# A hybrid encoder layer on one core: twelve of the sixteen gate products in the input stage instead of seven

## The chip, the cores and the metric

The kernel runs on one core of one Trainium2 chip. The time is device microseconds of one execution. A core has a matrix engine (PE, its weight loads shown as PEld), three engines for elementwise work (DVE, ACT, POOL) and a sync engine (SP) that mainly starts DMA transfers. Each engine takes its own instructions strictly in the order in which the program lists them, and waits where an operand is not there yet.

## What is computed

One encoder layer over two sequences of 1024 and 256 tokens, 1280 columns in all, with model width 1024. From the normalized input `h` one wide product `h @ w_in` gives the inputs of three things: attention, a recurrent branch (a scan over tokens in both directions) and 2048 gate columns. The change concerns the gate columns.

```
p = h @ w_in[l]
p_mla, p_rwkv, p_gate = (columns of p)
o_mla = mla_branch(p_mla, ...) @ w_mla_o[l]
o_rwkv = rwkv_branch(p_rwkv, ...) @ w_rwkv_o[l]      # holds the scan over tokens
gm, gr = jnp.split(jax.nn.sigmoid(p_gate), 2, axis=-1)
x = x + g1 * ((gm * o_mla + gr * o_rwkv) @ w_out[l])
...                                                  # then a SwiGLU feed-forward layer
```

The 2048 gate columns are 16 products of 128 columns each (8 for `gm`, 8 for `gr`). Each product has 8 slices of the contracted dimension, and each slice is multiplied three times, because a number is split into a high and a low half: high by high, high by low, low by high.

## The kernel before

The stages follow one another on PE: the input products (gemm, L67), attention, the scan with other work laid into it, the merge of the two branches, and the feed-forward layer. The order of every engine's instructions is fixed when the program is built, by a scheduler that runs through an estimated timeline (`schedule_with_timeline_sim=True`); the source order and the pools of buffers are its input. The rows of an execution say how long that order really takes.

The gate products are made in two places, and a constant `NB` (L35) divides them:

- `gates` (L443), called at L1369 behind the input products, makes products 0 to NB-1 from `h` as it lies in SBUF. It goes through the columns in chunks of 512, 512 and 256 (`CH`), so a product has 24 matmuls of 512 columns twice and 24 of 256 columns: 72. All use one PSUM buffer (`gps`, one bank), which ACT empties with a tanh (L456) before the next chunk may begin. The weights come in two halves per product; each is loaded (L51), cast on ACT (`whi`, L53) and subtracted on POOL (`wlo`, L55).
- `phase_fill` (L1131) makes products NB to 15 beside the scan, with `product` (L1044, matmuls at L1054). There `h` is read back from DRAM in pieces of 256 columns (`x`), so a product has 5 x 24 = 120 matmuls of 256 columns, and its weights are loaded and split once for each pass over the columns, three times in all. When the gates are done, the same function multiplies the attention output by `w_mla_o` (`mla_out`: loads `om` and the row sums `rs` into `raw` and `bc`, splits them, multiplies, and writes `xm` to DRAM). All of this together is called the fill below.

```
js = range(NB, 16)
ws = weights(g, io["w_in"][20 + NB], KT)
...
both = js[:LAG] if len(xs) > 1 else []
for j in both:
    gate(j, *xs, ws=ws)
```

The scan (`phase_rwkv`, L714) has ten batches of 128 tokens, each with two steps of 64 (`step`, L918). A step is a chain through PE and back: `py` (L927), copies to `ru`, `py` again with an inverted block `tt` (L933), copies to `xv`, the state update `pS` (L939) and the output (L945). `prepare` (L968; matmuls `pA`, L819) and `solve`/`invert` (L851, L1009) make the blocks of later batches. Steps have the highest priority in the scheduler, the inversions a smaller one, the rest none. Behind the scan `merge` (L1104) reads `xm` and the gates back.

Of the kernel before, what the change touches and what calls it, by code (L numbers as in the profile page):

```python
# [31 lines left out]
    VEC[_n] = (_at, _w)  # L32
    _at += _w
NVEC = _at
NB = 7  # L35
SPN = ('kk',)
WV = (0, 1)
AB = 8
# [8 lines left out]
def split_w(g, src, kt, eng=None, tag="w", pool=None, width=P, rbufs=2, bufs=2):  # L47
    nc = g.nc
    pool = pool or g.wst
    raw = pool.tile([P, kt, width], F32, tag=tag + "raw", name="wraw", bufs=rbufs)  # L50
    nc.sync.dma_start(out=raw if len(src.shape) == 3 else raw.rearrange("p (d f) n -> p d f n", d=src.shape[1]), in_=src)  # L51
    hi = pool.tile([P, kt, width], F32R, tag=tag + "hi", name="whi", bufs=bufs)
    nc.scalar.copy(hi, raw)  # L53
    lo = pool.tile([P, kt, width], F32R, tag=tag + "lo", name="wlo", bufs=bufs)
    (eng or nc.gpsimd).tensor_tensor(lo, raw, hi, ALU.subtract)  # L55
    return hi, lo
# [386 lines left out]
def gates(g, hh, hl):  # L443

    nc, io = g.nc, g.io
    for j in range(NB):
        ws = [split_w(g, io["w_in"][20 + j][:, k0:k0 + 4, :], 4, pool=g.gp, tag="gw", rbufs=1) for k0 in (0, 4)]
# [592 lines left out]
def weights(g, src, kt):  # L1040
    return [split_w(g, src[:, k0:k0 + 4, :], 4, pool=g.fl, tag=g.ft, rbufs=RB, bufs=WB) for k0 in range(0, kt, 4)]
# [89 lines left out]
def phase_fill(g):  # L1131
# [23 lines left out]

    js = range(NB, 16)
    ws = weights(g, io["w_in"][20 + NB], KT)
    spans = [(0, 256), (512, 768), (1024,)]
# [313 lines left out]
```

## Time and profile before

| what | value |
|---|---|
| time, median of 3 runs | 2715.98 us (2709.65 to 2723.69) |
| the profiled execution: its own time | 2719.07 us |
| its span, first to last instruction | 2717.4 us |
| PE busy | 2547.4 us, 94% |
| DVE, ACT, POOL busy | 1326.4, 1020.0, 841.7 us (49%, 38%, 31%) |
| mean granted TensorE clock | 0.957 of full speed |

A share of busy time is a mean over stages with different limits, so the stages are looked at one by one. A busy PE is one whose pipelined matmuls overlap: a 512-column matmul is shown with about 390 ns, but the next one starts about 230 ns later, and it is the distance between starts that counts.

### The profile page before, as it was taken

The numbers are of one execution on the slowest core, as the hardware profiler recorded it, in microseconds if no ns is written. First come the engines' busy times: TensorE is split into PE (matmuls) and PEld (weight loads), VectorE is DVE, ScalarE is ACT, GpSimd is POOL, SyncE is SP. The second block draws the span as 40 slices with busy tenths as digits, with TensorE's granted clock in tenths as the row PEclk, the third lists the DMA queues.
The fourth block names the chain that finished last, engine by engine and source line by source line (L and its number), as shares of the span: only waits on it lengthen the run. The fifth ranks groups of instructions, "written<-read, shape, count | busy, mean of one in ns | idle before, by whom it ended". The sixth has DMA issues, their size and how long they took to land.

```text
span 2717.4 us, 47321 instructions
## 1 busy us (share of the span) xinstructions
PE 2547.4 (94%) x19578; PEld 2160.1 (79%) x19578; DVE 1326.4 (49%) x2138; ACT 1020.0 (38%) x1913; POOL 841.7 (31%) x824
## 2 busy tenths in 40 slices
PE   5999999989997899999998988999999999999997
PEld 3777778778886788988877767778888888888886
DVE  6665562367776374565646557462222222222228
ACT  4433333257676565565653233241110111101114
POOL 1112131011115455454634466342111111111123
PEclk8999999999998798998988989999999999999998
DMA  7655531110013334444445655221111110111113
GB/s 294 226 185 198 188 146 63 45 29 18 20 32 107 103 107 137 141 114 137 126 147 164 191 182 154 92 71 55 39 39 39 39 36 35 39 39 39 39 40 132
DMA packets 178120, 273.80 MB, mean 101 GB/s; under 512 B 15008, under 2 KB 104944, under 8 KB 177904
## 3 DMA queue, kind: packets, MB, share of 16 engines
q1 hardware_dynamic: 164512, 223.19, 25.8%
q0 software_dynamic: 5760, 26.22, 2.4%
q10 hardware_dynamic: 7632, 21.37, 2.3%
q8 instruction: 154, 2.52, 0.4%
q14 instruction: 62, 0.51, 0.1%
HBM read 202.52 MB, written 68.20 MB: 100 GB/s over the span
## 4 chain that ended last, share of the span: by engine, by line
PE 75%; DVE 11%; ACT 5%; DMA 4%; issue 3%; POOL 2%; SPq 0%; DVEq 0%; POOLq 0%; ACTq 0%
PE mm L67 42%; PE fp L1054 8%; PE s L626 3%; PE o L660 2%; PE gps L453 2%; PE pA L819 2%; PE proj L559 2%; PE t L647 2%; PE py L927 2%; DMA ld<-scr_s 1%; PE pS L939 1%; PE py L945 1%; PE lora L369 1%; PE ada_ps L170 1%; PE py L933 1%
## 5 line engine op out<-in xcount | busy, mean ns | idle before, releaser
L55 POOL TENSOR_TENSOR wlo<-wraw,whi 128x512 fp32r<-128x512 f32 (+3 forms) x233 | 406.5, 1748 | 1177.6 <-ACT whi L53 1166.7
L53 ACT CAST whi<-wraw 128x512 fp32r<-128x512 f32 (+2 forms) x248 | 194.5, 789 | 898.0 <-issue 466.7
L67 PE MATMUL mm<-h2h,whi 128*128 128x512 f32 (+1 forms) x1056 | 279.2, 358 | 2.9 <-ACT whi L53 2.9
L67 PE MATMUL mm<-h2h,wlo 128*128 128x512 f32 (+1 forms) x1056 | 278.4, 357 | 1.1 <-POOL wlo L55 1.1
L67 PE MATMUL mm<-h2l,whi 128*128 128x512 f32 (+1 forms) x1056 | 278.2, 357 | 0.0
L67 PE MATMUL mm<-g,whi 128*128 128x512 f32 (+1 forms) x1056 | 240.6, 359 | 6.2 <-DVE ft L1259 5.6
L1054 PE MATMUL fp<-x,whi 128*128 128x256 f32 (+1 forms) x912 | 211.1, 324 | 11.7 <-ACT x L1036 5.0
L67 PEld LDWEIGHTS mm<-g,whi 128*128 128x128 f32 x1056 | 177.8, 190 | 38.0 <-issue 5.7
L67 PEld LDWEIGHTS mm<-h2h,whi 128*128 128x128 f32 x1056 | 177.1, 189 | 34.6 <-ACT whi L53 3.4
L67 PEld LDWEIGHTS mm<-h2h,wlo 128*128 128x128 f32 x1056 | 176.8, 188 | 32.7 <-POOL wlo L55 2.0
L67 PEld LDWEIGHTS mm<-h2l,whi 128*128 128x128 f32 x1056 | 176.9, 188 | 31.2 <-issue 0.5
L1271 DVE SCALAR_TENSOR_TENSOR x<-mm,g2h,x 128x512 f32<-128x512 f32 (+1 forms) x144 | 87.0, 655 | 196.3 <-PE mm L67 196.0
L1054 PEld LDWEIGHTS fp<-x,whi 128*128 128x128 f32 x912 | 157.6, 206 | 23.9 <-ACT x L1036 6.1
L67 PE MATMUL mm<-hl,whi 128*128 128x512 f32 (+1 forms) x480 | 147.5, 364 | 7.7 <-DVE hl L265 7.7
L67 PE MATMUL mm<-hh,whi 128*128 128x512 f32 (+1 forms) x480 | 148.1, 366 | 6.4 <-ACT pp L320 3.8
L1054 PE MATMUL fp<-x,wlo 128*128 128x256 f32 (+1 forms) x456 | 147.8, 325 | 6.3 <-POOL wlo L55 6.3
L1259 DVE SCALAR_TENSOR_TENSOR ft<-ft,mm 128x512 f32<-128x512 f32 (+1 forms) x66 | 36.0, 594 | 225.6 <-ACT ft L1258 225.6
L67 PE MATMUL mm<-hh,wlo 128*128 128x512 f32 (+1 forms) x480 | 145.8, 363 | 0.0
L1260 DVE TENSOR_TENSOR ft<-ft,mm 128x512 f32<-128x512 f32 (+1 forms) x66 | 36.0, 593 | 217.5 <-PE mm L67 217.5
L67 PE MATMUL mm<-g,wlo 128*128 128x512 f32 (+1 forms) x528 | 136.2, 359 | 1.4 <-POOL wlo L55 1.4
L626 PE MATMUL s<-kb,q 128*128 128x512 f32 (+1 forms) x432 | 112.0, 392 | 2.3 <-ACT pr L632 2.2
L67 PEld LDWEIGHTS mm<-hh,whi 128*128 128x128 f32 x480 | 84.5, 191 | 27.8 <-issue 6.9
(331 smaller groups left out, 5239.2 us busy)
## 6 DMA issues: line engine op xcount, KB each, us to landing
wraw<-in_w_ffn_in_dram SPq DMA_DIRECT2D x56, 512.0 KB, 3.5
wraw<-in_w_in_dram SPq DMA_DIRECT2D x68, 256.0 KB, 3.6
araw<-in_w_ada_dram ACTq DMA_DIRECT2D x32, 512.0 KB, 3.6
wraw<-in_w_ffn_out_dram SPq DMA_DIRECT2D x26, 512.0 KB, 3.6
wraw<-in_w_in_dram SPq DMA_DIRECT2D x20, 512.0 KB, 3.8
x<-scr_h SPq DMA_DIRECT2D x20, 512.0 KB, 7.5
araw<-in_w_ada_dram SPq DMA_DIRECT2D x16, 512.0 KB, 9.3
gt<-scr_gate SPq DMA_DIRECT2D x32, 256.0 KB, 2.7
```

The source lines that it names most:

```text
L53: nc.scalar.copy(hi, raw)
L55: (eng or nc.gpsimd).tensor_tensor(lo, raw, hi, ALU.subtract)
L67: nc.tensor.matmul(p[:, :n], lhsT=ww[:, k, :], rhs=aa[:, k, c0:c0 + n], start=(k == 0 and i == 0), stop=(k == kt - 1 and i == 2))
L453: nc.tensor.matmul(p[:, :n], lhsT=ww[:, k % 4, :], rhs=aa[:, k, c0:c0 + n], start=(k == 0 and i == 0), stop=(k == KT - 1 and i == 2))
L559: nc.tensor.matmul(p[:, :n], lhsT=ww[:, k, :], rhs=aa[:, k, c0:c0 + n], start=(k == 0 and i == 0), stop=(k == kt - 1 and i == 2))
L626: nc.tensor.matmul(s[:, o:o + w], lhsT=a[:, tt * P:(tt + 1) * P], rhs=b[:, c0 + o:c0 + o + w], start=(m == 0), stop=(m == 2))
L647: nc.tensor.transpose(t[:, j, :], prs[i][:, kk * P:(kk + 1) * P], g.ident)
L660: nc.tensor.matmul(o, lhsT=vs[h // 4][:, c0 // P + kk, h % 4, :], rhs=pts[j][m][kk // 4][:, kk % 4, :], start=(kk == 0 and m == 0), stop=( ...
L819: nc.tensor.matmul(pA[e][:, pt], lhsT=bk[HV[e], 2 * pt + sl], rhs=lt[HV[e], pt, e], start=True, stop=True)
L927: nc.tensor.matmul(py[e][HV[r], c, :], lhsT=lt[:, HV[r]], rhs=xv[:, u, e, :], start=(u == 0), stop=(r == 0 and u == 7))
L1054: g.nc.tensor.matmul(p[:, c:c + n], lhsT=ww[:, k % 4, :], rhs=aa[:, k, :n], start=(k == 0 and i == 0), stop=(k == kt - 1 and i == 2))
L1271: nc.vector.scalar_tensor_tensor(x1[:, dt, c0:c0 + n], p[:, :n], g.g2h[:, dt, c0 // TP:c0 // TP + 1], x1[:, dt, c0:c0 + n], ALU.mult, ALU.add)
```

## The change

```
-NB = 7
+NB = 12
```

Products 7 to 11 leave `phase_fill` and are made in `gates`. No other line is touched. In the changed program `gates` has 360 more matmuls (5 x 72) and `phase_fill` 600 fewer (5 x 120). What follows shows where the scheduler put them.

On SP, at the end of the input stage, between the tables for the attention keys (`ktab`) and queries (`qtab`), stand the weight loads of the last gate products:

```order
 L481 DMA ktab<-in_ktab_dram 64x1024
 L482 DMA ktab<-in_ktab_dram 64x256
-L51 DMA wraw<-in_w_in_dram 128x512 x3
+L51 DMA wraw<-in_w_in_dram 128x512 x13
 L538 DMA qtab<-in_qtab_dram 128x1024
 L51 DMA wraw<-in_w_uq_dram 128x384
```

Ten loads are added in one place, two for each of the five products. On PE the same holds: the last run of L453 matmuls ahead of attention had 144 in a row, which is two products, and now has 504, which is seven; all the earlier ones stand where they stood.

On PE, in the second step of the scan's sixth batch (`tt` is the inverted block, `py` and `pS` the step's products, `pA`, `pT`, `pv` those of `prepare`, `pz` of `invert`), the rows before are:

```order
L819 MATMUL pA<-lt,bk 128x128 x8
L832 MATMUL pT<-cst,bk 128x128 x4
L1054 MATMUL fp<-x,whi 128x256 x2
L927 MATMUL py<-xv,lt 64x64 x32
L840 MATMUL pv<-cst,ld 128x128 x4
L1054 MATMUL fp<-x,wlo 128x256
L1054 MATMUL fp<-x,whi 128x256 x2
L1054 MATMUL fp<-x,wlo 128x256
```

The same step in the changed program:

```order
L819 MATMUL pA<-lt,bk 128x128 x8
L832 MATMUL pT<-cst,bk 128x128 x4
L927 MATMUL py<-xv,lt 64x64 x32
L840 MATMUL pv<-cst,ld 128x128 x4
L840 MATMUL pv<-cst,vr 128x128 x4
L878 MATMUL pz<-xr,aa 32x16 x11
L933 MATMUL py<-ru,tt_8102 64x64 x8
```

The fill is gone from this step, and from every later one: in the changed program the last matmul of the fill (gates and `mla_out` together) stands just ahead of L933 in the first step of the sixth batch, while before it goes on to the end of the scan. Up to there the two programs have much the same number of fill matmuls in each step; what was the later gates is now `mla_out`, three batches earlier.

## Rows read from the trace of the kernel before

**Rows 1.** The page: span, and busy time of each engine.

```profile
span 2717.4 us, 47321 instructions
PE 2547.4 (94%) x19578; PEld 2160.1 (79%) x19578; DVE 1326.4 (49%) x2138; ACT 1020.0 (38%) x1913; POOL 841.7 (31%) x824
```

**Rows 2.** Busy time by stretch; behind POOL: granted clock, DMA share, GB/s.

```profile
0.00:514.00 514.00, 470.84 (x2550) 366.35 (x2551) 281.06 (x327) 186.02 (x269) 102.15 (x137) 0.98 0.48 174
514.00:549.04 35.04, 29.86 (x146) 23.29 (x145) 1.69 (x2) 5.89 (x9) 4.48 (x3) 1.00 0.16 56
870.00:924.00 54.00, 39.32 (x482) 34.94 (x482) 22.79 (x54) 29.99 (x71) 28.24 (x42) 0.78 0.55 164
924.00:1260.00 336.00, 320.70 (x4949) 293.91 (x4948) 186.72 (x389) 202.69 (x451) 170.33 (x232) 0.90 0.40 117
1260.00:1529.00 269.00, 250.67 (x3807) 219.68 (x3808) 150.62 (x272) 135.44 (x283) 126.37 (x145) 0.91 0.49 149
```

**Rows 3.** The same, of L453 alone (PE, PEld, clock, DMA share, GB/s).

```profile
514.00:549.04 35.04, 29.83 (x144) 23.25 (x144) 1.00 0.16 56
```

**Rows 4.** PE in order of time, inside those two products.

```profile
521.79 0.40 PE L453 MATMUL gps<-hl,whi 128*128 128x512 f32 x1
522.02 0.39 PE L453 MATMUL gps<-hh,wlo 128*128 128x512 f32 x1
...
527.87 0.39 PE L453 MATMUL gps<-hh,whi 128*128 128x256 f32 x1 [0.69 <-ACT gate L456]
528.09 0.28 PE L453 MATMUL gps<-hl,whi 128*128 128x256 f32 x1
528.21 0.28 PE L453 MATMUL gps<-hh,wlo 128*128 128x256 f32 x1
...
536.39 0.50 PE L453 MATMUL gps<-hh,wlo 128*128 128x512 f32 x1 [0.62 <-POOL wlo L55]
```

**Rows 5.** Chain that ended last, by line: first 924 to 1260, then 1260 to 1529.

```profile
by line: PE fp L1054 20.0%; PE pA L819 9.8%; DMA ld<-scr_s 7.3%; PE py L927 6.6%; PE py L945 4.1%; PE pS L939 3.8%; issue 3.8%; ACT xv L843 3.8%; DVE lt L806 3.2%; DVE L L773 2.8%; PE pw L891 2.6%; PE py L933 2.6%; PE pw L896 2.5%; PE pT L8
by line: PE fp L1054 17.3%; PE py L927 9.6%; issue 9.0%; PE pS L939 5.8%; PE py L933 5.6%; PE py L945 5.1%; PE pA L819 4.3%; DVE xt L864 4.3%; DVE W L866 2.5%; DVE x L1037 1.9%; ACT lt L826 1.7%; DMA bc<-scr_rs 1.7%; ACT xv L843 1.6%; PE pz
```

**Rows 6.** L927 over the scan: count, durations, first and last start.

```profile
L927 PE MATMUL py<-xv,lt x1280: 222/222/370, 924.1 to 1517.5; 128*64 128x64 f32 x183
```

**Rows 7.** Chain that ended last, in the sixth batch's first step.

```profile
1260.10 1.39 PE py L933 x16
```

**Rows 8.** L1054 alone by stretch (PE, PEld, clock, DMA share, GB/s).

```profile
1005.00:1260.00 255.00, 91.56 (x623) 82.05 (x622) 0.93 0.42 125
1260.00:1529.00 269.00, 99.66 (x495) 76.23 (x496) 0.91 0.49 149
```

**Rows 9.** The chain at the end of the scan.

```profile
1524.71 2.85 DMA scr_xm<-gt
...
1527.58 2.77 DMA xm<-scr_xm
```

**Rows 10.** Busy time in two stretches with a low clock (columns as in rows 2).

```profile
900.00:950.00 50.00, 41.05 (x564) 35.65 (x565) 17.16 (x43) 22.30 (x50) 17.83 (x29) 0.66 0.23 70
1366.60:1387.10 20.50, 18.93 (x141) 14.33 (x142) 11.62 (x21) 10.18 (x23) 10.03 (x16) 0.50 0.40 127
```

**Rows 11.** PE in order of time: L927 in that second stretch and behind it.

```profile
1382.91 3.31 PE L927 MATMUL py<-xv,lt 128*64 128x64 f32 x32
...
1402.37 1.85 PE L927 MATMUL py<-xv,lt 128*64 128x64 f32 x28
```

**Rows 12.** The chain while `mla_out` runs.

```profile
1368.56 4.52 DMA bc<-scr_rs
...
1375.20 1.78 DVE x L1037
...
1412.61 12.23 issue
```

**Rows 13.** PE in order of time: a wait of the fill there.

```profile
1427.41 0.50 PE L1054 MATMUL fp<-x,wlo 128*128 128x512 f32 x1 [2.42 <-POOL wlo L55]
```

## The prediction

> **What bounds the kernel now.** I read the page first: PE is busy for 94% of the span, and no other engine for more than half [rows 1]. So a change that moves PE work from one stage to another is worth what PE's time is worth in the two stages. Next comes the table by stretch. In the input stage, up to 514 us, PE is busy 471 of 514 us; its idle 43 us lie in pieces in which the old program already has the first gates. Then come 35 us with nothing but the last two gate products: DVE is busy 1.7 us there, ACT 5.9, POOL 4.5 [rows 2]. In that stretch PE alone sets the time.
>
> In the scan, from 924 to 1529 us, PE is busy 95% and 93% of the time, the others at 47 to 61% [rows 2]. That looks like a PE bound too, but a scan step is a chain that goes through PE, ACT and DVE and back, and PE takes its instructions in order, so fill matmuls in front of a step's matmul can be what makes PE full. Two views must be told apart. The view of one line says how much of PE the fill takes: 99.7 us of the 269 from 1260 on [rows 8]. The chain that ended last says how much of that stood in the way: L1054 has 20.0% of it up to 1260 and 17.3% behind that [rows 5]. About half of the fill's PE time lies in gaps that the scan leaves anyway.
>
> **The change, part by part.** *Added: five products at the end of the input stage.* The old trace has exactly this piece of program twice: 144 matmuls of L453, alone on PE, take 35.04 us [rows 3], which is 17.5 us a product. It can be rebuilt from single rows: 512-column matmuls start 0.23 us apart and 256-column ones 0.12 us [rows 4], so 24 x (0.23 + 0.23 + 0.12) = 13.9 us; the rest, 3.6 us, is PE waiting three times a product for ACT to empty the only PSUM buffer, and once or twice for POOL's low half of the weights (0.6 to 0.7 us each time in these rows) and starting up again behind it. The changed order has the five new ones back to back behind these two, with nothing else between, so 5 x 17.5 = **+87.6 us**. Nothing can hide it: attention starts behind it on PE. Two loads and two splits a product are added for SP, ACT and POOL; ACT's and POOL's 6 and 4 us of 35 leave room.
>
> [...] The row says: the granted clock is 1.00 over the two products [rows 2, 3], although PE stops at every change of chunk. [...]
>
> *Removed: the fill behind the sixth batch.* L927 has 1280 records, 128 for each of ten batches, and the sixth batch's first L933 starts at 1260.1 [rows 6, 7]. Up to that place the two programs have nearly the same number of fill matmuls per step, so I take the scan up to 1260 as unchanged, except for the waits named below. Behind it the old program has 269 us with 17.3% fill on the chain, 46.5 us. What only feeds the fill goes too: `bc` 1.7% (4.6 us), the low half of `x` 1.9% (5.1 us), and "issue", which is 9.0% here against 3.8% before [rows 5], so 5.2%, 14.0 us; its largest piece, 12.2 us at 1412.6, stands where PE then waits for a weight split behind the join's loads [rows 12, 13]. Together **-70.2 us**. Taking pieces out of a chain leaves a chain that still has to be run, in the same order of PE; so with the order kept this is about the most that can be won.
>
> *Moved: `mla_out` comes three batches earlier*, in place of gates, and brings its own loads and splits along: `bc` 4.6 and `x` 5.1 us, **+9.7 us**. The 14 us of issue I leave out, since the join, which held up POOL, stays where it is.
>
> *The end of the scan.* Before, `xm` is written and read back after the last scan step, 2.85 + 2.77 us on the chain [rows 9]. Now it has long been written: **-5.6 us**. The merge behind it has the same PE rows as before.
>
> *The clock.* Without fill PE will have gaps. Where it had them before, the granted clock fell: 0.78 between attention and the first step, 0.66 from 900 to 950 [rows 2, 10], and 0.50 for 20 us behind 1366.6. At 0.50, 32 records of L927 took 3.31 us; at full clock 28 took 1.85 us [rows 11]: 103 against 66 ns each. The scan's own main PE lines hold 9.6 + 5.8 + 5.6 + 5.1 + 4.3 = 30.4% of the late chain [rows 5], 81.8 us at a mean clock of 0.91. At 0.78 they grow by 0.91/0.78 - 1 = 17%, **+13.6 us**; the bounds are 0 and, at 0.66, 31.0 us. I take 0.78, because a stretch with prepare and inversion but few fill matmuls is what that row is.
>
> Sum: 87.6 - 70.2 + 9.7 - 5.6 + 13.6 = **+35 us**. The profiled execution took 2719.07 us, 3.1 above the median of the runs; 2719.1 + 35.1 = 2754, and as a median **2751 us**.
>
> **The rivals.** *PE bounds the scan also without the fill (the other side).* Then all 99.7 us that the fill took of PE come back, not the 70 of the chain, because the scheduler can lay prepare's and the inversion's matmuls into the gaps: 87.6 - 99.7 - 5.6 = -17.7, a median of 2698 (`mla_out`'s feeds would be hidden in such a scan). For it speaks PE at 93%; against it that DVE alone has 150.6 us in this stretch [rows 2] and only 169 would remain, in a chain of dependent steps. With the 5.6 us of the end, it is no loss from the point where the last 269 us shrink to 187, and a gain of over 0.5% below 173.
>
> *Another chain takes over.* The waits behind the fill become waits for something else: `ld<-scr_s`, 7.3% of the early chain [rows 5], which DVE waits for in order, or the inversion. Half of the 70.2 is won, and the clock falls to 0.66: 87.6 - 35.1 + 9.7 - 5.6 + 31.0 = +87.6, a median of 2804.
>
> *The input block is shorter than its model*, because with the weights split well ahead and the PSUM handovers hidden a product is only its 13.9 us: 5 x 3.6 = 18 us less, a median of 2733. The order shows the same one-buffer pattern, so this is unlikely.
>
> [...]
>
> **How the numbers follow.** Runs of this kernel differ by 0.5% between lowest and highest; less than 0.5%, 13.6 us, I call no change. Chances: the forecast 0.56, with its own range of 2725 to 2780 (the clock's bounds, and the issue term back or not); PE bound 0.14; another chain 0.20; shorter block 0.07; swinging clock 0.03. The range 2704 to 2800 leaves out the better part of the PE-bound case (0.08), some half of the other chain's (0.09) and the swinging clock (0.03). Faster by over 0.5%: 0.08, the lower part of the PE-bound case. Within 0.5%: 0.14, its rest (0.06), half of the shorter block (0.04), and the low end of the forecast (0.04). Slower: 0.78.
>
> **What would show it.** Right: in the changed profile L453's last run is seven products long and takes about 122 us, at clock 1.00; attention starts some 88 us later and takes as long as before; the scan's first L927 to its sixth batch takes about as long as before (336 us, with up to ten more); from the sixth batch's first L933 to the last L945 it takes about 212 us (269 - 70.2 + 13.6) with a granted clock well under 0.91; L1054 is nearly gone from the late chain. Wrong: the late scan takes under 187 us, or over 240; the new products cost other than 17 to 18 us each; the early scan slows by more than 20 us through `mla_out`'s loads; or the merge starts with a new wait.

## The result, and the profile after

The changed kernel takes 2810.47 us (median of 4 runs, 2806.97 to 2814.97) against 2719.84 us before (4 runs): a ratio of 1.034, with a 95% interval of 1.0305 to 1.0375. The forecast was 2751 us, the range reached to 2800. The profiled execution has a span of 2813.3 us, 95.9 more than before.

The page: span and busy time of each engine, the lines that answer to [rows 1].

```profile
span 2813.3 us, 46709 instructions
PE 2598.8 (92%) x19338; PEld 2190.9 (78%) x19338; DVE 1304.9 (46%) x2138; ACT 1012.1 (36%) x1893; POOL 817.3 (29%) x804
```

PE has 240 instructions less (360 matmuls more in the input stage, 600 fewer beside the scan) and yet 51 us more busy time. Matmuls that take longer are a first hint of a lower clock, which the stretches below bear out: 0.86 and 0.70 over the two parts of the scan, where it was 0.90 and 0.91.

Busy time by stretch of the changed kernel, as in [rows 2]: the last run of gate products, the scan up to the sixth batch's first L933, and the scan from there to the end of the last L945. Behind POOL stand the granted clock, the DMA share and GB/s.

```profile
514.00:642.70 128.70, 108.92 (x526) 84.30 (x526) 4.62 (x4) 20.51 (x36) 18.80 (x14) 1.00 0.18 63
1016.50:1396.90 380.40, 356.00 (x4851) 312.30 (x4850) 206.94 (x426) 209.93 (x462) 188.39 (x250) 0.86 0.49 145
1396.90:1633.00 236.10, 196.36 (x3314) 179.56 (x3313) 109.25 (x241) 108.82 (x229) 70.24 (x98) 0.70 0.21 60
```

Before, the same two parts of the scan took 336.0 us (924.1 to 1260.1) [rows 2] and 268.6 us (1260.1 to 1528.7), of which this is the row, with L1054 alone behind it:

```profile
1260.10:1528.70 268.60, 250.37 (x3805) 219.37 (x3805) 150.60 (x272) 135.06 (x281) 126.33 (x144) 0.91 0.49 149
1260.10:1528.70 268.60, 99.36 (x493) 75.93 (x493) 0.91 0.49 149
```

I call the two parts the early and the late part. In the changed kernel the early part is 44.4 us longer, and the late part, which has no fill left, is only 32.5 us shorter, at a clock of 0.70 against 0.91.

L1054 alone in the two parts, as in [rows 8] (PE, PEld, clock, DMA share, GB/s), the changed kernel first:

```profile
1016.50:1396.90 380.40, 134.97 (x667) 110.15 (x667) 0.86 0.49 145
1396.90:1633.00 236.10, 0.07 (x1) 0.07 (x1) 0.70 0.21 60
```

and the kernel before in its early part:

```profile
924.10:1260.10 336.00, 115.79 (x764) 103.51 (x764) 0.90 0.40 117
```

PE in order of time inside the run of seven products, as in [rows 4]:

```profile
542.49 0.50 PE L453 MATMUL gps<-hh,whi 128*128 128x512 f32 x1 [0.69 <-ACT gate L456]
...
560.51 0.50 PE L453 MATMUL gps<-hh,whi 128*128 128x512 f32 x1 [0.69 <-ACT gate L456]
```

From the second chunk of one product to that of the next it is 18.0 us, at a clock of 1.00. Over the whole run (516.99 to 642.51, where PE goes on to L559) the seven products take 125.5 us, against 35.0 for the two of before: 18.1 us for each of the five.

The chain by line, as in [rows 5], early part and late part:

```profile
by line: PE fp L1054 21.0%; PE pA L819 9.6%; PE py L927 5.8%; DMA ld<-scr_s 5.2%; issue 3.9%; PE py L945 3.8%; PE pT L832 3.2%; PE pS L939 2.9%; DMA bc<-scr_rs 2.7%; DVE L L773 2.5%; POOL bk L788 2.5%; DVE lt L806 2.5%; PE pw L896 2.2%; PE 
by line: issue 14.5%; PE py L927 11.7%; PE py L933 7.4%; PE pA L819 7.3%; DMA ld<-scr_s 6.2%; PE pS L939 5.5%; PE py L945 5.5%; PE pw L896 2.5%; PE pT L832 2.2%; DVE L L773 2.1%; PE pw L891 2.1%; DVE lt L806 1.9%; PE pz L878 1.8%; PE pz L88
```

L1054 is gone from the late chain, as forecast. What took its place is not one line: the shares of "issue", L927, L933 and L819 are larger than in the late chain before [rows 5], that of L939 is smaller (5.5% against 5.8%).

### The profile page after: what moved, and what is told of

The parts are those of the page before. It is cut to its first block, busy times and chain, and to the rows that moved or that the text cites. A ratio compares the mean times of both kernels' runs of the same rounds, so it can differ in the third digit from the quotient of the medians.

```text
span 2813.3 us, 46709 instructions
## 1 busy us (share of the span) xinstructions
PE 2598.8 (92%) x19338; PEld 2190.9 (78%) x19338; DVE 1304.9 (46%) x2138; ACT 1012.1 (36%) x1893; POOL 817.3 (29%) x804
## 4 chain that ended last, share of the span: by engine, by line
PE 72%; DVE 12%; DMA 5%; ACT 4%; issue 4%; POOL 3%; SPq 0%; POOLq 0%; DVEq 0%; ACTq 0%
PE mm L67 41%; PE fp L1054 6%; PE gps L453 4%; PE s L626 3%; PE pA L819 2%; PE o L660 2%; PE proj L559 2%; PE py L927 2%; PE t L647 2%; DMA ld<-scr_s 2%; POOL wlo L55 1%; PE py L945 1%; PE ada_ps L170 1%; PE lora L369 1%; PE py L933 1%
## 5 line engine op out<-in xcount | busy, mean ns | idle before, releaser
L55 POOL TENSOR_TENSOR wlo<-wraw,whi 128x512 fp32r<-128x512 f32 (+2 forms) x213 | 380.6, 1789 | 1211.8 <-ACT whi L53 1208.2
L53 ACT CAST whi<-wraw 128x1024 fp32r<-128x1024 f32 (+3 forms) x228 | 183.0, 804 | 909.5 <-issue 447.8
L1054 PE MATMUL fp<-x,whi 128*128 128x256 f32 (+1 forms) x512 | 136.9, 357 | 5.7 <-ACT x L1036 3.3
L453 PE MATMUL gps<-hh,whi 128*128 128x512 f32 (+1 forms) x288 | 106.3, 369 | 23.5 <-ACT gate L456 19.4
L1054 PEld LDWEIGHTS fp<-x,whi 128*128 128x128 f32 x512 | 98.6, 223 | 16.9 <-ACT x L1036 5.0
L819 PE MATMUL pA<-lt,bk 64*128 64x128 f32 x640 | 101.8, 337 | 10.0 <-ACT arb L828 6.2
```

The lines of the kernel that those rows point to most:

```text
L453: nc.tensor.matmul(p[:, :n], lhsT=ww[:, k % 4, :], rhs=aa[:, k, c0:c0 + n], start=(k == 0 and i == 0), stop=(k == KT - 1 and i == 2))
L819: nc.tensor.matmul(pA[e][:, pt], lhsT=bk[HV[e], 2 * pt + sl], rhs=lt[HV[e], pt, e], start=True, stop=True)
L1054: g.nc.tensor.matmul(p[:, c:c + n], lhsT=ww[:, k % 4, :], rhs=aa[:, k, :n], start=(k == 0 and i == 0), stop=(k == kt - 1 and i == 2))
```

## The experiments

To read them, the time of a part of the scan is split in three: what L1054 or an added matmul takes of PE (fill), what is left of PE's busy time (the scan's own), and PE's idle time. PE's busy time comes from the view by stretch, the fill's part from the view of its line, and the scan's own part is the difference of the two. In the kernel before the late part is 99.4 + 151.0 + 18.2 = 268.6 us, in the changed one 0.1 + 196.3 + 39.7 = 236.1. Where a fill matmul and one of the scan overlap, this puts the time down to the fill.

**The scan's side alone.** The function `gates` makes products 0 to 6, the fill 12 to 15. Products 7 to 11 are left out, and where their gates are read, those of other products stand in (two reads, not shown).

```
 def gates(g, hh, hl):
 ...
-    for j in range(NB):
+    for j in range(7):
```

> The scan's side alone: gates makes products 0 to 6 as before, phase_fill makes only 12 to 15. Products 7 to 11 are left out (other products' gates are read in their place), so this is the changed kernel without its longer input block. Theory A (the forecast's: the fill stood on the scan's chain): 2720 - 52 = about 2665 us. Theory B (the scan is no shorter without the fill, since its clock falls and mla_out comes early): the changed kernel less its input block of 92 us, about 2718 us, no different from before.

Measured: 2724.3 us, ratio to before 1.0018 (0.9991 to 1.0045), no change. Its two parts, by stretch:

```profile
930.80:1309.80 379.00, 349.56 (x4851) 306.54 (x4851) 203.38 (x426) 206.48 (x456) 187.37 (x246) 0.86 0.49 145
1309.80:1545.70 235.90, 196.12 (x3313) 178.76 (x3313) 108.67 (x241) 109.14 (x229) 69.05 (x98) 0.73 0.22 61
```

These are 379 and 236 us, as in the changed kernel. To have five gate products fewer beside the scan, in this order, is worth nothing; the loss of the change is about its input block. Theory A falls, B holds for the total.

**Idle matmuls behind `mla_out`.** To the changed kernel, 600 matmuls of 256 columns are added that need no load and feed nothing, so that PE has work in batches six to nine as before. The function `idle_work` (not shown) makes a constant tile and multiplies it into the fill's PSUM buffers, here 25 times 24 matmuls.

```
     mla_out(*((x, *c) for x, c in zip(as_, CH[1:])))
+    idle_work(25)
```

> The changed kernel with 600 matmuls of 256 columns added to phase_fill behind mla_out, on a constant tile: no weights, no loads, and nothing reads them. The scheduler lays them into batches six to nine; up to there PE's order is that of the changed kernel. Theory B (an empty PE loses its clock and that costs what the fill cost): 2800 to 2815 us, no more than the changed kernel, with a granted clock above 0.9 in batches six to nine and late scan time, from the sixth batch's first L933 to the last L945, of 235 us or less. Theory A (PE time of the fill stands on the chain): 46 us more than the changed kernel, about 2855 us, late scan time about 280 us.

Measured: 2822.15 us, 1.0392 (1.0376 to 1.0409): 12 us over the changed kernel, neither the 46 of theory A nor quite the none of theory B. Its late part, in all and (second row, by line: PE, PEld, clock, DMA, GB/s) the idle matmuls alone:

```profile
1387.50:1635.70 248.20, 236.31 (x3876) 222.09 (x3875) 110.39 (x240) 109.08 (x228) 67.03 (x97) 0.90 0.22 60
1387.50:1635.70 248.20, 81.94 (x563) 75.62 (x562) 0.90 0.22 60
```

The clock is back at 0.90, and the scan's own PE time falls from 196.3 to 236.3 - 81.9 = 154.4 us. PE's idle time falls from 39.7 to 11.9. So 82 us of useless matmuls cost 12 us: 42 came back in the scan's own time and 28 went into gaps. (The scan's own records, taken by themselves, cover 161.3 us; so 35 of the 42 us hold however overlaps are counted.) That the 42 us belong to the clock can be seen from a product: own time times clock is 151.0 x 0.91 = 137 us before, 196.3 x 0.70 = 137 in the changed kernel, and 154.4 x 0.90 = 139 here (143 and 147 in the two small doses further down). One batch shows it best. By stretch, the seventh batch of three kernels: first the kernel before (L1054 has 18.55 us of its PE time), second the changed kernel, which has no fill there, third this run, in which the idle matmuls take 26.36 us of PE's.

```profile
1303.20:1359.90 56.70, 53.11 (x926) 49.31 (x924) 38.76 (x67) 39.71 (x89) 37.01 (x46) 0.97 0.46 132
```

```profile
1440.60:1505.20 64.60, 55.77 (x794) 50.15 (x792) 28.38 (x70) 31.57 (x71) 21.69 (x34) 0.63 0.21 58
```

```profile
1435.50:1502.70 67.20, 65.81 (x962) 61.45 (x960) 29.94 (x74) 31.36 (x70) 21.60 (x34) 0.85 0.22 60
```

Without any fill, at a clock of 0.63, the batch keeps PE busier than with it at 0.97, 55.8 against 53.1 us, and takes 7.9 us longer.

**Idle matmuls ahead of `mla_out`.** The same 600, between the gates and `mla_out`, which is thereby as late as before the change.

```
+    idle_work(25)
     a = pair(1, 4, 512)
     scaled(a, *CH[0])
```

> The changed kernel with the same 600 matmuls between the gates and mla_out, so that mla_out is back in batches seven to ten, where the kernel before has it, and the gate products are still four. Theory M (the early scan is longer because mla_out and its loads stand in it): first L927 to the sixth batch's first L933 falls from about 381 to 335 to 345 us, and the total to 2790 to 2805 us. Theory X (it is longer because four gate products instead of nine bring the two reloads of the input pieces closer together): the early scan stays at 375 or more, and the total is 2830 or more.

Measured: 2829.47 us, 1.0419 (1.0398 to 1.0440). The early part takes 355.6 us (1017.3 to 1372.9), between the two theories. The total is close to theory X's (2830 or more) and 19 us above the changed kernel: the late part, with `mla_out` back in it, takes 269.9 us, 33.8 more. The first batch varies by itself: it took 83.0 us in the changed kernel and 75.5 in the run with the idle matmuls late, which has the same PE order there. So I compare from the second batch's first L927 to the sixth's:

| kernel | second to sixth batch, us | `mla_out` there |
|---|---|---|
| before | 239.0 (1005.1 to 1244.1) | no |
| changed | 281.9 (1099.5 to 1381.4) | yes |
| the scan's side alone | 278.5 (1013.8 to 1292.3) | yes |
| idle matmuls late | 276.9 (1093.4 to 1370.3) | yes |
| idle matmuls ahead of `mla_out` | 251.9 (1101.9 to 1353.8) | no |
| idle matmuls spread (below) | 245.6 (1105.3 to 1350.9) | no |

Of the 43 us, 30 go when `mla_out` goes and idle matmuls of 256 columns stand in its place. So what theory M names carries most of the early loss, X at most the rest.

**Idle matmuls spread as the gate products were.** 240 in each of the first two passes, 120 in the third, on the pass's own `x`.

```
         for j in both:
             gate(j, *xs, ws=ws)
             ws = None
+        idle_work(xs, 5 * len(xs))
```

> The changed kernel with the 600 idle matmuls spread as the five gate products were in the kernel before: 240 in each of the first two passes over the columns and 120 in the third, each on the pass's own piece of the input, so that the reloads of the pieces stand as far apart as before and mla_out as late as before. What it lacks of the fill before is the five products' weights and outputs. Theory X+M (the early scan is longer for these two reasons and no other): early scan 333 to 343 us, late 262 to 272 us, total 2805 to 2817 us. If the weights, the ten loads and splits less a pass, matter: shorter than that. If the spacing of the reloads is nothing: early scan 350 us or more, as with the idle matmuls ahead of mla_out.

Measured: 2814.32 us, 1.0328 (1.0286 to 1.0369): as the changed kernel. Early part 350.5 us, late 261.2. The total was as expected, the early part some 8 us over, of which the first batch (87.5 us against 81.0 before) has 6.5. With the reloads apart the early batches are another 6 us shorter; runs with the same order there differ by 5 us (281.9 and 276.9 in the table), so this shows little.

**The stores of y on another queue.** In the changed kernel's late part a store of the scan's output stands ahead of the next batch's loads on SP and waits for ACT, and the chain goes through it (ACT's copy `yt` at 1472.90, the start of the store at 1474.22, a load of the next batch at 1474.92). If that chain were what had taken the fill's place, moving the stores should shorten the scan.

```
-            nc.sync.dma_start(out=g.scr[f"y{d}"][t:t + 64, :], in_=bt.yt[HV[st], 4 * d:4 * d + 4])
+            nc.scalar.dma_start(out=g.scr[f"y{d}"][t:t + 64, :], in_=bt.yt[HV[st], 4 * d:4 * d + 4])
```

> The changed kernel with the stores of the scan's output y (L952) started from ACT's queue instead of SP's. Theory Q (in the changed kernel a store of y that waits for ACT stands at the head of SP's queue, the next batch's loads wait behind it, and that chain has taken the fill's place): late scan time falls from 236 to 215 to 222 us and the total to 2785 to 2797 us. Theory C (the low clock alone has taken the fill's place): late scan time 232 us or more, total 2803 to 2815 us.

Measured: 2806.72 us, 1.0296 (1.0260 to 1.0333); late part 230.9 us. What SP waited for in the late part, before the move and (second fence) after it (total us, times, longest):

```profile
SPq L952 <- ACT yt L949: 72.5, 8, 17.7
SPq L754 <- DVE lt L806: 62.3, 4, 30.8
```

```profile
SPq L754 <- DVE lt L806: 75.2, 4, 35.8
```

The 72.5 us of waiting are gone. The late part of the profiled execution is 5 us shorter, but that execution was the fastest of its four (2799.16 us), and the medians differ by 4 us; so a gain is not shown. The total lies in theory C's range, and theory Q falls: the loads wait for the buffers that DVE has not yet freed, 75.2 us instead of 62.3.

The same move in the kernel before:

> The kernel before with the same move of the stores of y to ACT's queue. There SP waits 23 us for these stores from 1260 us on and 22 us ahead of that. Theory Q: the scan gets 10 to 25 us shorter, total 2693 to 2708 us. If the fill stands on the chain in any case: no change, 2712 to 2722 us.

Measured: 2743.63 us, 1.0071 (1.0048 to 1.0094), 0.7% longer. Its early part is 362.0 us against 336.0, at a clock of 0.85 against 0.90. Both expectations were wrong. A move of a few stores, with the same PE work, made the early part 26 us longer; why is not shown.

The move together with the 600 idle matmuls behind `mla_out`:

> The changed kernel with the stores of y on ACT's queue and the 600 idle matmuls behind mla_out. Beside the run with the stores moved alone it shows what the clock is worth once SP's queue is out of the way. Theory C (what the fill takes of PE it gives back through the clock): within 8 us of that run, clock above 0.85 in batches six to nine against 0.6 to 0.75. Theory A: 20 us or more longer than that run.

Measured: 2820.41 us, 1.0349 (1.0307 to 1.0390), 14 us over the run with the move alone, between the theories and much as the 12 us without the move: the queue makes no difference that can be seen to what a filled PE costs. The clock of the late part is 0.90, against 0.73 in the run with the move alone; of batches seven to nine it is 0.85, 0.99 and 0.90, against 0.63, 0.75 and 0.81.

**A small dose.** 20 idle matmuls ahead of each state update from the seventh batch on, 140 in all, then 60 each.

```
+            for _ in range(20 if sv.n > 5 else 0):
+                nc.tensor.matmul(psn.rearrange("p u m -> p (u m)")[:, :256], lhsT=idle[:, 0, :], rhs=idle, start=True, stop=True)
             for u, _, e, _, _, bkt in ops:
                 nc.tensor.matmul(psn[HV[e], u, :], lhsT=bkt, rhs=xv[:, u, e, :], start=True, stop=True)
```

> The changed kernel with 20 idle matmuls of 256 columns (a constant tile; 2.4 us at full clock) into the state update's PSUM buffer ahead of each state update, from the seventh batch on: 140 in all, laid where PE waits within a step or beside it. It is a small dose against the 600 of before. Theory C (the empty scan is long because its clock has fallen): the clock of the last four batches rises from 0.7 to 0.8 or more, the late scan time falls from 236 to 222 us or less, total 2785 to 2800 us. Theory W (the clock is low because PE waits, and the waits set the length): 236 to 245 us, total 2808 to 2825 us.

Measured: 2821.02 us, 1.0355 (1.0320 to 1.0390). The late part, in all and (second row) the idle matmuls alone:

```profile
1388.20:1630.80 242.60, 204.62 (x3453) 187.76 (x3453) 108.76 (x241) 109.03 (x229) 68.88 (x98) 0.79 0.21 59
1388.20:1630.80 242.60, 23.73 (x140) 21.83 (x140) 0.79 0.21 59
```

> The same with 60 idle matmuls ahead of each state update, 7.2 us at full clock, 420 in all. Theory C: the clock reaches 0.9, the late scan time is 225 to 240 us, since what the clock gives is about what the matmuls take. Theory W: the matmuls add to the waits, 250 us or more.

Measured: 2854.66 us, 1.0474 (1.0436 to 1.0513); late part 279.5 us at a clock of 0.79. The small dose lifted the clock from 0.70 to 0.79 and took 15 us off the scan's own PE time (204.6 - 23.7 = 180.9), but it took 24 us itself, and PE's idle time stayed at 38 us. Theory C had the clock about right and the time wrong; theory W had the time right for both doses. The larger dose did not lift the clock further: its 420 matmuls took 57.8 us, and the scan's own part was 186.7 us. So placed, idle matmuls cost about their own time less what the clock gave back. That W's reason, the waits within the steps, sets the length is not shown.

**Other divisions.** `NB` set to 9, 6 and 5.

> NB = 9: two products more in gates than before. If the scan is as long with any amount of fill (what the experiments so far say), only the input block counts: 2 x 18 = 36 us, 2750 to 2765 us. By the forecast's own terms, two fifths of its 35 us: 2725 to 2740 us.

Measured: 2739.82 us, 1.0074 (1.0048 to 1.0101): the upper end of the second expectation, by the forecast's own terms. The last gate matmul ends 38.7 us later than before, and the scan is shorter here, 334.1 + 251.3 us:

```profile
964.60:1298.70 334.10, 312.21 (x4913) 286.62 (x4911) 184.15 (x389) 205.79 (x458) 177.42 (x238) 0.91 0.43 124
1298.70:1550.00 251.30, 226.25 (x3601) 198.86 (x3601) 140.60 (x277) 124.63 (x258) 103.93 (x126) 0.90 0.46 136
```

The early part is as before: the first matmul of `mla_out` with 512 columns stands at 1306.0, behind it. The late part, with 67.8 us of L1054, has kept its clock and is 17 us shorter. So "any amount of fill" was too much said: the first two products that leave give about half of their 38.7 us back. The next three give another 15 us in the late part, and the early part grows by 46.

> NB = 6: one product more beside the scan than before. The input block is 18 us shorter. If fill is free as long as it ends with the scan: 2700 to 2710 us. If a product more runs on behind the scan, as two did with NB = 5: 2715 to 2745 us.

Measured: 2741.51 us, 1.0053 (1.0022 to 1.0083), within the second expectation. The profiled execution, the longest of five (2750.20 us), has a scan of 646 us (910.1 to 1556.6), 42 more than before; the fill's last matmul starts at 1562, and what comes behind the scan is only 3 us longer. So one product more lengthened the scan itself, other than expected.

> The change turned round: NB = 5, so that two products more stand beside the scan than before. The input block gets 2 x 18 = 36 us shorter. Theory B (fill is nearly free where it keeps PE's clock up): 2685 to 2700 us. Theory A (each product in the fill costs its 14.4 us of PE time, most of it on the chain): 2705 to 2715 us; if mla_out then runs on behind the scan, 2715 or more.

Measured: 2756.18 us, 1.0155 (1.0128 to 1.0181), far above theory B's range; only the last case of theory A, that `mla_out` runs on, came. The scan takes 621.5 us (892.0 to 1513.5), 17 more than before; `mla_out` runs on until 1569, and what comes behind the scan takes 1240 us instead of 1189. Fill is not free here. None of the versions run beat the kernel before.

## Why the prediction was wrong

The sign was right, and the size was off by a factor of 2.6 (90.6 us between the medians, 35 forecast), outside the range. Term by term, from the two profiled executions:

| term | forecast, us | measured, us |
|---|---|---|
| five products in the input stage | +87.6 | +93.5 (642.7 - 549.2) |
| attention, up to the first L927 | 0 | -1.1 |
| the scan up to the sixth batch's first L933 | +9.7 | +44.4 |
| the scan behind it | -70.2 + 13.6 = -56.6 | -32.5 |
| behind the scan | -5.6 | -8.4 |
| sum | +35.1 | +95.9 |

*The input block* was right within 6 us. A product is 18.1 us where the model had 17.5, and the block starts 3 us later. So the shorter block, 13.9 us a product, did not come. No run shows a clock that swings in this block, the case with 0.03 of the chances: it was 1.00 over the 128.7 us of the block, with 32 stops of PE of 0.35 to 1.22 us each in it, as it had been over the 35.0 us of the two products before.

*"I take the scan up to 1260 as unchanged" failed*, by 35 us, the largest error. The step rested on the count of fill matmuls in each batch. But the gates' matmuls in the fill have 256 columns, and most of `mla_out`'s have 512, which start 0.23 us apart instead of 0.12 at full clock, as in [rows 4]. By L1054's rows, 667 matmuls took 135.0 us in the early part, where 764 had taken 115.8: the count was not the same either, but 192 of the 667 have 512 columns, so that together they have 12% more columns than the 764. These 19 us of fill are the first piece of the 44. The others are the scan's own PE time at a clock of 0.86 instead of 0.90 (204.8 to 221.0 us) and 9 us of PE's idle time, about what the forecast had for the new waits (9.7). The forecast had named an early scan more than 20 us longer through `mla_out`'s loads as a sign of being wrong; it came, but more through PE's matmuls than through waits. With `mla_out` moved out of the early part by idle matmuls, 30 of 43 us went. `mla_out` also comes earlier than the three batches that the forecast says: its first matmul with 512 columns stands at 1367.4 before, in the eighth batch, and at 1222.1 now, at the end of the third.

*The clock was under-priced.* The term took a clock of 0.78 and only the five lines that the old chain showed, 81.8 us. The clock fell to 0.70, and the scan's own PE time, 151.0 us, became 196.3, that is 45 us more, against 13.6 forecast. The idle matmuls show that this part belongs to the clock: with them the clock was 0.90 and the own time 154.4 us. How much of the 45 us is on the late part's length is not shown.

*The 14 us of "issue" were not the fill's.* The late chain has 14.5% issue now, 34 us, without any fill. Its largest piece is 26.4 us at 1576.7, in which POOL waits in the join, which stayed. The piece of 12.2 us in [rows 12] was of the same kind, POOL's wait for a load of the join; I read it as a wait of the fill, because a wait of the fill stood beside it. Before and now:

```profile
1424.87 1.26 POOL L1077 TENSOR_TENSOR y<-y,yb 128x512 f32<-128x512 f32 x1 [12.26 <-DMA yb<-scr_y]
1603.10 2.50 POOL L1100 TENSOR_TENSOR wg<-wg,bg 128x512 f32<-128x512 f32 x2 [26.41 <-DVE wg L1099]
```

*What was right in the late part*: removing a piece of a chain won at most that piece here; the fill's 99.4 us of PE were worth 33. By batches, the part of the sixth behind 1260.1 and the seventh, where the fill had been gates, became 0.6 and 7.9 us longer without it. The eighth to tenth, where it had been `mla_out`, became 41 us shorter, 127.8 instead of 168.8 (from the starts of L927). So the late part won where `mla_out` had stood, and the early part, into which it moved, lost 44.4.

The rival "another chain takes over" had the total nearly right (2804), with a clock of 0.66, but by luck: it has the early part 9.7 us longer where it was 44.4, and the late part 4 us shorter where it was 32.5. Its waits for loads were tried by moving the stores of y, without a gain that shows. The rival in which PE bounds the scan also without the fill would have given all 99.7 us back and did not come. PE is still 83% busy in the late part, with 39.7 us idle, because its own work takes longer at the lower clock (196.3 us at 0.70, where it took 151.0 at 0.91).

*What stays open.* How long the scan would be without fill and at full clock was not shown: each way that raised the clock also took PE time. So the runs show that clock and fill largely set each other off, and that the loss of clock is 42 to 45 us of PE time in the late part (35 to 37 if overlaps are not put down to the fill); they do not show that PE's time alone, and not the waits in the steps, sets the length. Why the larger small dose left the clock at 0.79 is open too, and so is why a fill of one product more (NB = 6) made the scan 42 us longer.

## What to carry to other kernels

Work beside a stretch of dependent steps can be paid for in part by the slots that the stretch leaves anyway and by the clock that it keeps up, as it was here, where 82 us of idle matmuls held the clock at 0.90 instead of 0.70 and cost 12 us; before moving it away, look for what the engine's own instructions cost at the clock of a stretch without it. When a schedule is compared by counts of instructions, weigh each by its width (here 667 matmuls, 192 of them of 512 columns, took 135.0 us where 764 of 256 had taken 115.8), and ask what moves up into the place of what left. Take a chain's share as the most that a removal may win with the rest unchanged, not as an estimate of it: here 70.2 us of pieces on the chain became 32.5.

## What the runs showed of the hardware that was not expected

Of 600 matmuls that no one needs, 563 lay in the late part, with 82 us of PE time, and the kernel was only 12 us longer: the granted clock went from 0.70 to 0.90 with them, the scan's own PE time fell by 42 us, and PE's idle time by 28. In the seventh batch PE was busy for 55.8 us with no fill at a clock of 0.63; the same batch before, with 18.6 us of fill at 0.97, had 53.1. In the input block of the changed kernel PE stopped 32 times, at changes of chunk or of weights, for 0.35 to 1.22 us and 1.4 to 6.4 us apart, and the clock was 1.00 for the 128.7 us.
